# The query rank as the first seven-product unit, with the sums of x partly on GpSimd and two norms moved into later units

## The chip, the cores and the metric

One core of a Trainium2 chip runs the kernel. The metric is the device time of one execution in microseconds (us). Three runs of the kernel before gave 1342.76, 1343.64 and 1344.71; the median is 1343.64. A difference under 0.2% (2.7 us) is about what a measurement of this kernel cannot tell from no change.

## The reference

A hybrid encoder block over 512 tokens of width 2048, float32 throughout. The part that the change touches is the input projection and the two norms that follow it:

```
h = rmsnorm(x, norm_w)
proj = h @ w_in                       # 2048 x 10128
a_q, a_f, a_i, a_g, c_q, c_kv, k_idx_raw, w_idx_raw, b_g, m_a, m_b = split(proj)
# widths: 4 x 1024, c_q 512 (queries' rank), c_kv 256, k_idx_raw 128, 16, 1024, 2 x 2048
cq = rmsnorm(c_q, q_norm_w)           # over 512
k_idx = layernorm(k_idx_raw, kidx_norm_w, kidx_norm_b)    # over 128
...                                   # cq and k_idx are used after all the gates are projected
```

## The kernel before

TensorE multiplies in a pair of fp32r numbers: every operand is split into a high part (ScalarE, a copy to fp32r) and a low part (VectorE, the operand minus its high part), and `mm3` issues three matmuls for each product: high by high, high by low, low by high. `split(hi, lo, src)` writes both parts. x is kept transposed and split in `xh` and `xl`, 16 blocks of 128 rows by 512 tokens.

There are two kinds of projection. `feat_job` is the plain one: it loads a block of weights (`wr`, 512 rows of w_in at a time, two raw buffers), splits it into `wh` and `wl`, and runs `mm3` with 512 tokens as the moving side. `pair_job` is a seven-product scheme (Strassen-Winograd) on 2x2 blocks: 512 features by 512 tokens by 256 rows of x for each block of weights. Of the four quarters of x it needs four sums (`s0` to `s7`, one tile for each pair of 128-row blocks, split in two like all else), of the weights four sums (`pair_sums`, lines 158 to 174: three additions on VectorE into `sv`, then the high parts `bh` and `wh` on ScalarE and the low parts `bl` and `wl` on VectorE). `pair_unit` runs eight blocks of 42 matmuls of 256 columns; its seven results stand in seven PSUM banks, and `pair_evac` puts them together: one ScalarE copy of the first product, then seven VectorE additions. The next unit's first product takes the bank that the ScalarE copy frees, its third to seventh those that the additions free.

There is no scheduler: instructions stand on each engine in the order in which the program is written. `prep(i)` prepares weights up to two blocks ahead of the block that TensorE is about to use. `pump()` is called after each 12 matmuls in a plain job and after each block of a pair unit; it issues the stores that are due and takes one step of every generator in `lanes` ("misc", "norm" and others). `load_ahead` issues the load of a weight block on SyncE's queue as soon as one of the two raw buffers is free by program order.

After `start()` (norm of x, transposes, the values of one head pair) the jobs come in this order: the first half of the queries' rank (`cq_evac(0)`, plain), the raw indexer keys (`kx_evac`), the second half of the rank, the keys' and values' rank (`ckv_evac`), then 13 seven-product units: 11 for the gates and 2 for `qf_d`. Beside the four plain jobs run `pair_gen`, which makes the eight `s` tiles (one pair in three pumps), and on the "norm" lane `q_sums` and `kidx_gen`, the sums of squares by a matmul with ones (`ns`) and the norms' factors (`rstd_row`: Ln and Exp on ScalarE, each behind a table load). `q_rows` scales and splits the rank later, in the third unit. The pools "norms" and "pairs" follow each other in the same memory: `open_pairs` finishes the two lanes and changes the pool when the first pair block is prepared.

Of the kernel before, what the change touches and what calls it, by code (L numbers as in the profile page):

```python
# [63 lines left out]
EVEN = 0  # L64
MO = (0, 128, 384, 768)
# [3 lines left out]
def hybrid_block(ctx, tc, x, norm_w, w_in, lb_table, gnorm_a, q_norm_w, kv_norm_w, w_uq,  # L69
# [51 lines left out]
    cq_d = dram.tile([4, 128, T], F32, name="cq_d")  # L121
    qf_d = dram.tile([2, 4, 128, T], F32, name="qf_d")
# [400 lines left out]
    def cq_evac(j0):  # L523
        def evac(c, ps):
            t = R.cq[:, j0 + c, :]
            A.activation(t, ps, AF.Copy)
            late[1].append(lambda: SP.dma_start(cq_d[j0 + c], t))
        return evac

    def kx_evac(c, ps):  # L530
        A.activation(R.kx[:, 0, :], ps, AF.Copy)

    def ckv_evac(c, ps):
        t = R.g.tile([128, 2, 256], F32, name=f"c{c}").rearrange("p a b -> p (a b)")
        A.activation(t, ps, AF.Copy)
        late[1].append(lambda: SP.dma_start(ckv_d[c], t))
# [7 lines left out]
    def q_sums(j0):  # L544

        for j in (j0, j0 + 1):
            s = R.i.tile([128, T], F32, name="nsq", bufs=2)
            A.activation(s, R.cq[:, j, :], AF.Square)
            if j == 0:
                R.qs = R.i.tile([128, T], F32, name="qs")  # L550
                first = s
            elif j == 1:
                V.tensor_add(R.qs, first, s)
            else:
                V.tensor_add(R.qs, R.qs, s)
        if j0 == 0:
            yield
            return
        sh = R.i.tile([128, T], FR, name="sumh")
        sl = R.i.tile([128, T], FR, name="suml")  # L560
        split(sh, sl, R.qs)
        yield
        yield
# [555 lines left out]
    def open_norms():  # L1119
# [8 lines left out]
        R.cq = R.i.tile([128, 4, T], F32, name="cq")  # L1128
        R.kx = R.i.tile([128, 1, T], F32, name="kx")
# [14 lines left out]
    def pair_gen():  # L1144
        for k in range(8):
            s = slice(2 * (k % 2), 2 * (k % 2) + 2)
            a = R.i.tile([128, 2, T], F32, name="sv", bufs=2)
            V.tensor_tensor(a, xh[k // 2][:, s, :].bitcast(F32), xl[k // 2][:, s, :].bitcast(F32), op=OP.add)
            a11, a21, a12, a22 = (a[:, i, j:j + 256] for i in (0, 1) for j in (0, 256))
            d = R.i.tile([128, 4, 256], F32, name="sv", bufs=2)  # L1150
# [14 lines left out]
            if k == EVEN:  # L1165
                split(hi4, lo4, df[:, 768:])
# [499 lines left out]
```

## Time and profile before

| | |
|---|---|
| median of three runs | 1343.64 us (1342.76 to 1344.71) |
| the profiled execution | 1345.55 us, span of its instructions 1343.8 us |
| TensorE busy | 1331.4 us, 99% of the span |
| VectorE busy | 1088.4 us, 81% |
| ScalarE busy | 691.4 us, 51% |
| GpSimd busy | 51.7 us, 4%; none between 1.6 and 624 us |
| DMA | 150 GB/s, 202.10 MB |
| first plain job starts | 42.43 us |
| first seven-product unit starts | 120.40 us |
| thirteenth ends | 616.12 us |

Times are in us from the first instruction. A busy share is that of instructions in flight; matmuls overlap, so a TensorE at 99% has no wait, but says nothing of the time of one matmul. That is read from the length of a job divided by its matmuls.

### The profile page before, as it was taken

How to read it: one execution, taken by the hardware profiler on the slowest of the kernel's cores; microseconds unless marked ns; L12 is line 12 of the kernel's file. 1: busy time of each engine (PE TensorE's matmuls, PEld its weight loads, DVE VectorE, ACT ScalarE, POOL GpSimd, SP SyncE). 2: the span in 40 equal slices, each digit the busy share in tenths (PEclk: the TensorE clock that was granted, in tenths of full speed). 3: DMA queues.
4: the chain of work that ended last, by engine and by line, in shares of the span. 5: the costliest groups of instructions: out<-in, count | busy, mean ns of one | idle time of the engine just before them, and what ended most of it. 6: DMA issues, size and time to landing. Idle time of an engine off the chain costs nothing.

```text
span 1343.8 us, 27088 instructions
## 1 busy us (share of the span) xinstructions
PE 1331.4 (99%) x11058; PEld 1243.0 (93%) x11058; DVE 1088.4 (81%) x1764; ACT 691.4 (51%) x1115; POOL 51.7 (4%) x63
## 2 busy tenths in 40 slices
PE   8999999999999999999999999999999999999997
PEld 8888999999999999999999898888888888899996
DVE  7978889988898888886778887975656658899997
ACT  7555445545554445445756554655433434354455
POOL 0000000000000000000000000020101100001112
PEclk9999999999999999999999999999999999999999
DMA  7245345544453454446214433445856556654643
GB/s 226 71 118 145 108 142 173 158 141 142 127 154 105 138 154 142 143 143 207 85 51 140 132 106 96 126 136 172 289 167 202 181 187 212 212 174 148 194 145 126
DMA packets 143326, 202.10 MB, mean 150 GB/s; under 512 B 10545, under 2 KB 83810, under 8 KB 143074
## 3 DMA queue, kind: packets, MB, share of 16 engines
q1 hardware_dynamic: 142914, 200.12, 47.5%
q8 instruction: 86, 1.41, 0.4%
q14 instruction: 38, 0.31, 0.1%
q10 hardware_dynamic: 288, 0.26, 0.1%
HBM read 166.25 MB, written 35.66 MB: 150 GB/s over the span
## 4 chain that ended last, share of the span: by engine, by line
PE 97%; DVE 1%; DMA 0%; ACT 0%; issue 0%; SPq 0%; DVEq 0%; ACTq 0%
PE pp L94 16%; PE pp L95 16%; PE pp L96 16%; PE acc L94 14%; PE acc L96 13%; PE acc L95 13%; PE acc L99 2%; PE hl L99 1%; PE ho L99 1%; PE sc L94 1%; PE sc L95 1%; PE sc L96 1%; DMA x<-in_x_dram 0%; PE pt L374 0%; PE hp L99 0%; PE po L96 0%
## 5 line engine op out<-in xcount | busy, mean ns | idle before, releaser
L171 ACT ACTIVATE wh<-sv 128x512 fp32r<-128x512 f32 x264 | 158.6, 625 | 114.4 <-DVE sv L164 85.4
L169 ACT ACTIVATE bh<-wr 128x768 fp32r<-128x768 f32 x132 | 111.5, 845 | 197.6 <-issue 91.8
L95 PE MATMUL pp<-s,wh 128*128 128x256 f32 x624 | 172.6, 277 | 0.0
L94 PE MATMUL pp<-s,wh 128*128 128x256 f32 x624 | 172.6, 277 | 0.0
L96 PE MATMUL pp<-s,wl 128*128 128x256 f32 x624 | 172.6, 277 | 0.0
L173 DVE TENSOR_TENSOR wl<-sv,wh 128x1024 fp32r<-128x1024 f32 x132 | 161.2, 1221 | 5.4
L172 DVE TENSOR_TENSOR bl<-wr,bh 128x768 fp32r<-128x768 f32 x132 | 126.0, 954 | 37.7 <-ACT bh L169 37.3
L94 PE MATMUL acc<-xh,wh 128*128 128x512 f32 x304 | 121.0, 398 | 0.0
L96 PE MATMUL acc<-xh,wl 128*128 128x512 f32 x304 | 118.8, 391 | 0.0
L95 PE MATMUL acc<-xl,wh 128*128 128x512 f32 x304 | 118.6, 390 | 0.0
L95 PEld LDWEIGHTS pp<-s,wh 128*128 128x128 f32 x624 | 117.2, 188 | 0.0
L96 PEld LDWEIGHTS pp<-s,wl 128*128 128x128 f32 x624 | 117.2, 188 | 0.0
L94 PEld LDWEIGHTS pp<-s,wh 128*128 128x128 f32 x624 | 117.2, 188 | 0.0
L95 PE MATMUL pp<-xl,bh 128*128 128x256 f32 x416 | 115.1, 277 | 0.0
L96 PE MATMUL pp<-xh,bl 128*128 128x256 f32 x416 | 115.0, 277 | 0.0
L94 PE MATMUL pp<-xh,bh 128*128 128x256 f32 x416 | 115.0, 277 | 0.0
L91 DVE TENSOR_TENSOR wl<-wr,wh 128x1024 fp32r<-128x1024 f32 (+1 forms) x70 | 84.0, 1201 | 28.8 <-ACT wh L90 28.7
L90 ACT ACTIVATE wh<-wr 128x1024 fp32r<-128x1024 f32 (+1 forms) x70 | 72.3, 1033 | 61.6 <-PE acc L95 38.1
L164 DVE TENSOR_TENSOR sv<-wr 128x512 f32<-128x512 f32 x132 | 92.7, 702 | 10.3 <-DMA wr<-in_w_in_dram 6.9
L94 PE MATMUL acc<-yh,wh 128*128 128x512 f32 x256 | 100.3, 392 | 0.0
L96 PE MATMUL acc<-yh,wl 128*128 128x512 f32 x256 | 99.9, 390 | 0.0
L95 PE MATMUL acc<-yl,wh 128*128 128x512 f32 x256 | 99.9, 390 | 0.0
(391 smaller groups left out, 3769.9 us busy)
## 6 DMA issues: line engine op xcount, KB each, us to landing
wr<-in_w_in_dram SPq DMA_DIRECT2D x136, 512.0 KB, 3.7
wr<-in_w_out_dram SPq DMA_DIRECT2D x28, 512.0 KB, 3.9
mg<-gate_d SPq DMA_DIRECT2D x48, 256.0 KB, 5.3
gate_d<-c SPq DMA_DIRECT2D x44, 256.0 KB, 5.2
wr<-in_w_in_dram SPq DMA_DIRECT2D x36, 256.0 KB, 3.1
wr<-in_w_pa_dram SPq DMA_DIRECT2D x16, 512.0 KB, 5.4
wr<-in_w_pb_dram SPq DMA_DIRECT2D x16, 512.0 KB, 4.0
wr<-in_w_qidx_dram SPq DMA_DIRECT2D x8, 512.0 KB, 4.5
```

The costliest lines, as they stand in the source:

```text
L90: A.activation(hi, src, AF.Copy)
L91: V.tensor_tensor(lo, src, hi.bitcast(F32), op=OP.subtract)
L94: PE.matmul(ps, lh, rh, start=first, stop=False, skip_group_check=True)
L95: PE.matmul(ps, lh, rl, start=False, stop=False, skip_group_check=True)
L96: PE.matmul(ps, ll, rh, start=False, stop=last, skip_group_check=True)
L99: PE.matmul(ps, l, r, start=first, stop=last, skip_group_check=True)
L164: V.tensor_tensor(sv[:, 0:2, :], b[:, 1:3, :], b[:, 0:1, :].to_broadcast([128, 2, 256]), op=OP.add)
L169: A.activation(bh, b[:, 1:4, :], AF.Copy)
L171: A.activation(vh[:, i:i + 2, :], sv[:, i:i + 2, :], AF.Copy)
L172: V.tensor_tensor(bl, b[:, 1:4, :], bh.bitcast(F32), op=OP.subtract)
L173: V.tensor_tensor(vl, sv, vh.bitcast(F32), op=OP.subtract)
```

## The change

The four plain jobs of 256, 128, 256 and 256 features become two, the keys' and values' rank and the indexer keys; the queries' rank (512 features) becomes the first seven-product unit, ahead of the thirteen. `pair_gen` becomes two generators. `pair_early` makes six of the eight `s` tiles beside the two plain jobs, one pair in each pump: VectorE adds the two parts of x (`xa`) and makes the first sum, GpSimd makes the other three (`G.tensor_tensor`, 256 columns), and the split follows two steps later. `pair_late` makes the last two beside the first two blocks of the rank's unit, with two of four sums on GpSimd. The raw indexer keys go through memory (`kx_d`). `kidx_gen` and a new `q_squares` (which reads the rank back from `cq_d` to square and add it) run in the units after, followed by `q_rows`.

```diff
+EARLY = 6
...
     def kx_evac(c, ps):
-        A.activation(R.kx[:, 0, :], ps, AF.Copy)
+        t = R.g.tile([128, 2, 256], F32, name="c0").rearrange("p a b -> p (a b)")
+        A.activation(t, ps, AF.Copy)
+        SP.dma_start(kx_d, t)
...
+    def q_squares():
+        for j0 in (0, 2):
+            for _ in range(3):
+                yield
+            ts = [R.g.tile([128, 2, 256], F32, name=f"c{i}").rearrange("p a b -> p (a b)") for i in range(2)]
+            for i, t in enumerate(ts):
+                SP.dma_start(t, cq_d[j0 + i])
+            yield
+            yield
+            for t in ts:
+                A.activation(t, t, AF.Square)
...
+        sh, sl = R.cqh[:, 3, :], R.cql[:, 3, :]
+        split(sh, sl, R.rq)
+        yield
+        ps = row_sums(sh, sl)
+        rstd_row(ps, 512, R.rq)
+        for _ in range(7):
+            yield
...
     def kidx_gen():
+        t, parts = R.rq, (R.cqh[:, 2, :], R.cql[:, 2, :])
+        SP.dma_start(t, kx_d)
+        yield
+        yield
+        split(*parts, t)
+        yield
+        ps = row_sums(*parts)
+        V.scalar_tensor_tensor(t, ps, -1.0 / 128, t, op0=OP.mult, op1=OP.add)
+        yield
+        s = R.g.tile([128, 2, 256], F32, name="c3").rearrange("p a b -> p (a b)")
         A.activation(s, t, AF.Square)
+        split(*parts, s)
+        yield
+        rstd_row(row_sums(*parts), 128, s)
+        yield
+        V.scalar_tensor_tensor(t, t, c_iw, s, op0=OP.mult, op1=OP.mult)
         V.tensor_scalar(t, t, c_ib, None, op0=OP.add)
         split(R.kih, R.kil, t)
...
+    def pair_early():
+        made = []
+        for k in range(EARLY + 2):
+            if k > 1:
+                hi, hi4, lo, lo4 = sums_place(k - 2)
+                df = made.pop(0).rearrange("p q n -> p (q n)")
+                split(hi, lo, df[:, 0:768] if hi4 is not None else df)
...
+            if k < EARLY:
+                a = R.i.tile([128, 2, T], F32, name="xa", bufs=3)
+                V.tensor_tensor(a, *pair_rows(k), op=OP.add)
+                a11, a21, a12, a22 = (a[:, i, j:j + 256] for i in (0, 1) for j in (0, 256))
+                d = R.i.tile([128, 4, 256], F32, name="sv", bufs=3)
+                V.tensor_tensor(d[:, 0, :], a21, a22, op=OP.subtract)
+                G.tensor_tensor(d[:, 1, :], d[:, 0, :], a11, op=OP.subtract)
+                G.tensor_tensor(d[:, 2, :], a11, a21, op=OP.subtract)
+                G.tensor_tensor(d[:, 3, :], d[:, 1, :], a12, op=OP.add)
+                made.append(d)
+            yield
+
+    def pair_late():
+        for k in range(EARLY, 8):
+            ae, ao, da, db = (R.g.tile([128, 2, 256], F32, name=f"c{i}") for i in range(4))
+            for i, a in enumerate((ae, ao)):
+                V.tensor_tensor(a.rearrange("p a b -> p (a b)"), *(x[:, i, :] for x in pair_rows(k)), op=OP.add)
+            a11, a21, a12, a22 = (a[:, j, :] for a in (ae, ao) for j in (0, 1))
+            V.tensor_tensor(da[:, 0, :], a21, a22, op=OP.subtract)
+            V.tensor_tensor(da[:, 1, :], da[:, 0, :], a11, op=OP.subtract)
+            G.tensor_tensor(db[:, 0, :], a11, a21, op=OP.subtract)
+            G.tensor_tensor(db[:, 1, :], da[:, 1, :], a12, op=OP.add)
+            yield
+            hi, _, lo, _ = sums_place(k)
...
-    lane("misc", pair_gen)
-    feat_job(w_in, 4096, 2, NK, 4, x_rhs, cq_evac(0))
-    lane("norm", lambda: q_sums(0))
+    lane("misc", pair_early)
+    feat_job(w_in, 4608, 2, NK, 4, x_rhs, ckv_evac)
     feat_job(w_in, 4864, 1, NK, 4, x_rhs, kx_evac)
-    lane("norm", kidx_gen)
-    feat_job(w_in, 4352, 2, NK, 4, x_rhs, cq_evac(2))
-    lane("norm", lambda: q_sums(2))
-    feat_job(w_in, 4608, 2, NK, 4, x_rhs, ckv_evac)
+    lane("misc", pair_late)
+    pair_job(w_in, [4096, 4352], NK // 2, x_pair, pair_evac([cq_d[0:2], cq_d[2:4]], [None, None]))
+    for gen in (kidx_gen, q_squares, q_rows):
+        lane("norm", gen)
```

Line numbers move by two in the helpers: the split's low part is line 91 before and 92 after, the three matmuls 94 to 96 and 95 to 97. In the rows that follow, `wl<-wr,wh` is the low part of a weight block, `s<-sv,s` that of a sum of x, and `sv<-xh,xl` or `xa<-xh,xl` the two parts of x added.

The first place is VectorE from the first sum of x on, beside the first plain job. Before:

```order
L1148 TENSOR_TENSOR sv<-xh_92,xl_95 128x1024
L1151 TENSOR_TENSOR sv<-sv 128x256
L91 TENSOR_TENSOR wl<-wr,wh 128x1024
L1153 TENSOR_TENSOR sv<-sv 128x256
L1154 TENSOR_TENSOR sv<-sv 128x256
L1155 TENSOR_TENSOR sv<-sv 128x256
L91 TENSOR_TENSOR s_713<-sv,s_713 128x768
L91 TENSOR_TENSOR s_713<-sv,s_713 128x256
L91 TENSOR_TENSOR wl<-wr,wh 128x512
```

After, from the fourth pair's `xa` to the low part of the last block of the indexer keys:

```order
L1167 TENSOR_TENSOR xa<-xh_94,xl_97 128x1024
L1170 TENSOR_TENSOR sv<-xa 128x256
L92 TENSOR_TENSOR s_771<-sv,s_771 128x1024
L1167 TENSOR_TENSOR xa<-xh_92,xl_95 128x1024
L1170 TENSOR_TENSOR sv<-xa 128x256
L92 TENSOR_TENSOR wl<-wr,wh 128x512
L92 TENSOR_TENSOR s_801<-sv,s_801 128x1024
L1167 TENSOR_TENSOR xa<-xh_92,xl_95 128x1024
L1170 TENSOR_TENSOR sv<-xa 128x256
L92 TENSOR_TENSOR s_826<-sv,s_826 128x1024
L92 TENSOR_TENSOR wl<-wr,wh 128x512
L92 TENSOR_TENSOR s_849<-sv,s_849 128x1024
```

Three of four 256-column sums of a pair have left VectorE, and the weights' low parts of the indexer keys (128x512) now stand behind the sums of five and six pairs, where one or two stood ahead of them. The row behind the last is again `wl<-wr,wh 128x512`.

On GpSimd, whose queue held nothing between the start and the cast for the branches, stand the sums of the first pair, and the same three rows for each of the next five:

```order
L336 MEMSET rows 128x128
L1171 ISA
L1171 TENSOR_TENSOR sv<-sv,xa 128x256
L1172 TENSOR_TENSOR sv<-xa 128x256
L1173 TENSOR_TENSOR sv<-sv,xa 128x256
```

They came from VectorE's lines 1153 to 1155.

The second place is VectorE in the rank's unit, behind the weights of its third block (`sv<-wr` to `wl<-sv,wh` are one block's weights; `c` tiles hold the two halves of x and their sums, `s_1063` is the seventh pair's place):

```order
L1181 TENSOR_TENSOR c_996<-xh_92,xl_95 128x512
L1181 TENSOR_TENSOR c_997<-xh_92,xl_95 128x512
L1183 TENSOR_TENSOR c_998<-c_996,c_997 128x256
L1184 TENSOR_TENSOR c_998<-c_998,c_996 128x256
L166 TENSOR_TENSOR sv<-wr 128x512
L167 TENSOR_TENSOR sv<-sv,wr 128x256
L168 TENSOR_TENSOR sv<-sv,wr 128x256
L174 TENSOR_TENSOR bl<-wr,bh 128x768
L175 TENSOR_TENSOR wl<-sv,wh 128x1024
L92 TENSOR_TENSOR s_1063<-c_998,s_1063 128x512
L92 TENSOR_TENSOR s_1063<-c_999,s_1063 128x512
```

In units before only the five rows from `sv<-wr` on stood there; the four above and the two below are new, once for each of the two late pairs.

The third place is ScalarE in the first gate unit, from the sixth block on. Before, two blocks' weights (`bh`, `wh`) and the evacuation's copy (`c<-pp`):

```order
L169 ACTIVATE bh<-wr 128x768
L171 ACTIVATE wh<-sv 128x512 x2
L169 ACTIVATE bh<-wr 128x768
L171 ACTIVATE wh<-sv 128x512 x2
L1222 ACTIVATE c_1710<-pp 128x512
```

After:

```order
L537 ACT_TABLE_LOAD
L537 ACTIVATE c_1740<-ns,cols 128x512
L538 ACT_TABLE_LOAD
L538 ACTIVATE c_1740<-c_1740 128x512
L171 ACTIVATE bh<-wr 128x768
L173 ACTIVATE wh<-sv 128x512 x2
L91 ACTIVATE kih<-rq 128x512
L171 ACTIVATE bh<-wr 128x768
L173 ACTIVATE wh<-sv 128x512 x2
L1243 ACTIVATE c_1922<-pp 128x512
```

The factor of the indexer keys' norm, which stood beside the plain jobs, now stands ahead of the high parts of the next two weight blocks. It waits for the `ns` matmuls behind the unit's sixth block. Behind those weights on VectorE stand the norm's last three operations (lines 631, 632 and the low part `kil`), ahead of the unit's evacuation.

More of the change, by code (lines that the diff above doesn't have):

```diff
@@ L542, in rstd_row, with row_sums @@
         return r
[L544 to L553, printed above, removed]
-            else:
-                V.tensor_add(R.qs, R.qs, s)
-        if j0 == 0:
-            yield
[L558 to L563, printed above, removed]
+    def q_squares():
[9 more added lines that the diff above has]
+                A.activation(t, t, AF.Square)
+            if j0 == 0:
+                V.tensor_add(R.rq, *ts)
+            else:
+                V.tensor_add(ts[0], *ts)
+                V.tensor_add(R.rq, R.rq, ts[0])
+            for _ in range(3):
+                yield
[5 more added lines that the diff above has]
+        for _ in range(7):
+            yield
+    def row_sums(sh, sl):
         ps = bank("ns")
@@ new lines, in sums_place @@
+    def sums_place(k):
+        t = R.x.tile([128, 2048 + 64 * (k == EVEN)], FR, name=f"s{k}")
+        if k == EVEN:
+            parts = [t[:, 0:768], t[:, 784:1040], t[:, 1344:2112], t[:, 1040:1296]]
+        else:
+            parts = [t[:, 0:1024], None, t[:, 1024:2048], None]
+        for xs, a, b in ((xs_h, *parts[0:2]), (xs_l, *parts[2:4])):
+            cut = [a[:, i:i + 256] for i in range(0, 768, 256)]
+            xs.append(cut + [a[:, 768:1024] if b is None else b])
+        return parts
@@ new lines, in pair_rows @@
+    def pair_rows(k):
+        return (x[k // 2][:, 2 * (k % 2):2 * (k % 2) + 2, :].bitcast(F32) for x in (xh, xl))
+    def pair_early():
[5 more added lines that the diff above has]
+                split(hi, lo, df[:, 0:768] if hi4 is not None else df)
+                if hi4 is not None:
+                    split(hi4, lo4, df[:, 768:])
+            if k < EARLY:
[8 more added lines that the diff above has]
+                made.append(d)
+            yield
@@ new lines, in pair_late @@
+    def pair_late():
[8 more added lines that the diff above has]
+            G.tensor_tensor(db[:, 1, :], da[:, 1, :], a12, op=OP.add)
+            yield
+            hi, _, lo, _ = sums_place(k)
+            for i, d in enumerate((da, db)):
+                n = slice(i * 512, i * 512 + 512)
+                split(hi[:, n], lo[:, n], d.rearrange("p a b -> p (a b)"))
@@ L1231, in store @@
                 def store(c=c, f=f, t=t):
-                    A.activation(c, c, fn[f])
+                    if fn[f] is not None:
+                        A.activation(c, c, fn[f])
                     late[1].append(lambda: SP.dma_start(dst[f][:, :, t:t + 256].rearrange("f p t -> p f t"), c))
```

57 lines of the change are left out of this document (3 added, 54 removed).

## The prediction

> **What bounds the kernel now.** I read the page first, for the share of each engine and the chain that ended last:
>
> ```profile
> PE 1331.4 (99%) x11058; PEld 1243.0 (93%) x11058; DVE 1088.4 (81%) x1764; ACT 691.4 (51%) x1115; POOL 51.7 (4%) x63
> PE 97%; DVE 1%; DMA 0%; ACT 0%; issue 0%; SPq 0%; DVEq 0%; ACTq 0%
> ```
>
> TensorE never waits for long, so a matmul less is time less as long as the others keep up. Then the windows by stage: the first rank half, the indexer keys, the second half, the first unit and the third (the one with `q_rows`):
>
> ```profile
> core 0: us, PE busy (x) PEld busy (x) DVE busy (x) ACT busy (x) POOL busy (x), PEclk, DMA share, GB/s
> 42.43:64.21 21.78, 21.78 (x99) 18.04 (x97) 18.96 (x38) 10.43 (x18) 0.00 (x0) 1.00 0.25 64
> 64.21:75.10 10.89, 10.89 (x50) 9.03 (x49) 8.94 (x14) 5.98 (x8) 0.00 (x0) 1.00 0.58 171
> 75.10:97.90 22.80, 22.80 (x102) 18.84 (x101) 16.65 (x24) 13.09 (x16) 0.00 (x0) 1.00 0.39 112
> 120.40:158.53 38.13, 38.13 (x336) 38.12 (x335) 33.13 (x47) 18.69 (x30) 0.00 (x0) 1.00 0.51 149
> 196.66:234.80 38.14, 38.14 (x338) 38.14 (x337) 35.59 (x52) 19.11 (x32) 0.00 (x0) 1.00 0.50 153
> ```
>
> A plain job of 256 features takes 21.78 us for 96 matmuls (0.227 each), a unit 38.13 for 336 (0.1135 each, 4.77 a block). VectorE is busy for 33.13 of a unit's 38.13: it follows closely, and its queue, not its share, must be read next. The timeline of VectorE where the sums of x begin:
>
> ```profile
> 52.81 1.22 DVE L1148 TENSOR_TENSOR sv<-xh,xl 128x1024 f32<-128x1024 f32 x1
> 54.06 0.42 DVE L1151 TENSOR_TENSOR sv<-sv 128x256 f32<-128x256 f32 x1
> 54.41 1.22 DVE L91 TENSOR_TENSOR wl<-wr,wh 128x1024 fp32r<-128x1024 f32 x1
> 55.54 0.42 DVE L1153 TENSOR_TENSOR sv<-sv 128x256 f32<-128x256 f32 x1
> 57.20 1.29 DVE L91 TENSOR_TENSOR s<-sv,s 128x768 fp32r<-128x768 f32 x2 [0.45 <-ACT s L90]
> 58.42 0.68 DVE L91 TENSOR_TENSOR wl<-wr,wh 128x512 fp32r<-128x512 f32 x1
> 59.02 1.22 DVE L1148 TENSOR_TENSOR sv<-xh,xl 128x1024 f32<-128x1024 f32 x1
> ```
>
> Steps from start to start: 1.13 us for 1024 columns, 0.60 for 512, 0.35 for 256, 1.22 for 768 with 256, and 1.60 for `xa` with the sum that reads it. And VectorE at the end of the first unit (which ends at 158.53):
>
> ```profile
> 156.44 0.69 DVE L1223 TENSOR_TENSOR c<-pp,c 128x512 f32<-128x512 f32 x1
> 159.16 0.68 DVE L1227 TENSOR_TENSOR c<-pp,c 128x512 f32<-128x512 f32 x1
> 160.96 0.68 DVE L164 TENSOR_TENSOR sv<-wr 128x512 f32<-128x512 f32 x1
> 162.48 0.95 DVE L172 TENSOR_TENSOR bl<-wr,bh 128x768 fp32r<-128x768 f32 x1
> 163.35 1.22 DVE L173 TENSOR_TENSOR wl<-sv,wh 128x1024 fp32r<-128x1024 f32 x1
> 164.48 0.68 DVE L164 TENSOR_TENSOR sv<-wr 128x512 f32<-128x512 f32 x1
> ```
>
> One pair block of weights takes 3.52 (160.96 to 164.48), 2.39 of it to the end of `bl`; the evacuation takes 4.52 and begins 2.1 before the unit's end. The next unit's fifth product takes the bank that the fifth addition (L1227) frees. It is due 24 matmuls into the unit, at 158.53 + 2.72 = 161.25, and the addition ends at 159.84: 1.4 us of slack.
>
> **Matmuls.** Removed: two plain jobs, 2 x 21.78 = 43.56 (the 1.0 more of the second window are four `ns` matmuls, which only move). Added: one unit, 38.13. That is -5.43 us, all of it on the path, if TensorE isn't kept waiting. The rank's stores stay four; its evacuation and the two table loads of each norm stay in number.
>
> **VectorE up to the rank's unit.** Number the weight blocks 0 to 3 (keys' and values' rank), 4 to 7 (indexer keys), 8 to 15 (rank's unit), 16 on (gates). Up to 52.81 nothing changes. TensorE needs a low part at a block's third matmul: block 5 at 64.21 + 2.72 + 0.45 = 67.4, block 6 at 70.1, block 7 at 72.8; the `bl` of pair block 12 at 75.1 + 4 x 4.77 + 0.23 = 94.4. Ahead of block 7's low part VectorE now has six `xa` with their sum (6 x 1.60), the low parts of six sums (1.22 + 5 x 1.13) and five blocks (1.13 + 4 x 0.60): 20.0, so 72.8. Just in time, if GpSimd's 18 sums cost VectorE nothing.
>
> They don't come free. Where GpSimd's adds met VectorE late in this trace:
>
> ```profile
> 878.82 1.89 POOL L1012 TENSOR_TENSOR MB<-M,bh 128x256 f32<-128x256 f32 x2 [49.64 <-DMA bh<-bh_d]
> 878.86 1.25 DVE L816 TENSOR_TENSOR hq<-hq,tot 128x512 f32<-128x512 f32 x1
> 880.04 1.22 DVE L818 TENSOR_TENSOR hk<-hk,tot 128x512 f32<-128x512 f32 x1
> 880.68 0.90 POOL L1014 TENSOR_TENSOR MB<-M,bh 128x128 f32<-128x128 f32 x1
> 881.18 1.47 DVE L91 TENSOR_TENSOR wl<-wr,wh 128x1024 fp32r<-128x1024 f32 x1
> 881.54 1.72 POOL L1012 TENSOR_TENSOR MB<-M,bh 128x256 f32<-128x256 f32 x1
> 882.58 1.29 DVE L828 TENSOR_TENSOR tot<-tot 128x256 f32<-128x256 f32 x2
> 883.78 0.69 DVE L816 TENSOR_TENSOR hq<-hq,tot 128x512 f32<-128x512 f32 x1
> ```
> ```profile
> L1012 POOL TENSOR_TENSOR MB<-M,bh x24: 727/738/1721, 878.8 to 1060.3; 128x256 f32<-128x256 f32 x24
> ```
>
> The two take turns: L816 takes 1.25 beside a 256-column add, 0.69 without; L818, of the same shape, 1.22. Each such add stops VectorE for 0.53 to 0.56 us, more than the 0.35 that VectorE would need for the sum itself, and is stopped in turn (738 ns alone, up to 1721). I take 0.53, the lower, since some adds will fall into VectorE's own waits; the ends are 0, and 0.74 (the whole add).
>
> The Trainium skill's page "SBUF — State Buffer", section "Who interferes with whom", says that a VectorE instruction with two SBUF inputs and a GpSimd instruction that reads SBUF exclude each other, and that the loser blocks for the whole instruction. By that the cost would be 0.74 an add; the rows above show less, 0.53 to 0.56, and I go by them.
>
> So 18 x 0.53 = 9.5 on top. Walked down the queue, with one GpSimd add between every two VectorE operations: block 5's low part at 73.6 (6.2 us late), block 6's at 80.25 (3.9 more), then VectorE waits 1.1 for ScalarE's high part of the sixth sum, and block 7's is done at 83.7. The load of block 8 waits for block 6's low part (the raw buffer):
>
> ```profile
> wr<-in_w_in_dram SPq DMA_DIRECT2D x136, 512.0 KB, 3.7
> ```
>
> With 0.4 to issue it lands at 84.3. From there four blocks (14.1), the VectorE part of the two late pairs (2 x 2.0), the low parts of the seventh (1.2), block 12 to its `bl` (2.4) and four more adds (2.0): 108.0, against 94.4. TensorE is 13.6 us late. Without the stops the same walk gives block 6 at 70.95 (0.85 late), block 7 at 74.2, block 8's load at 75.0, and 96.7 for block 12: 2.3 us.
>
> **Unit boundaries.** From block 12 on VectorE has 1.1 + 1.2 (eighth pair) + 5 x 3.52 = 19.9 before the evacuation, TensorE 18.8 to the unit's end: the evacuation begins 1.1 after the end instead of 2.1 before it. Less the slack of 1.4 this holds the next unit for 1.8 us.
>
> In the first gate unit (blocks 16 to 23) the keys' norm meets the same edge. Its factor waits for `ns` matmuls behind block 21; the chain on ScalarE is that of the rank's norm before:
>
> ```profile
> 109.57 1.28 ACT L540 ACT_TABLE_LOAD   x1
> 110.86 0.69 ACT L540 ACTIVATE rq<-ns,cols 128x512 f32<-128x512 f32 x1
> 111.57 1.28 ACT L541 ACT_TABLE_LOAD   x1
> 112.86 0.63 ACT L541 ACTIVATE rq<-rq 128x512 f32<-128x512 f32 x1
> ```
>
> Behind it stand the high parts of block 24, which otherwise start when block 21 is done:
>
> ```profile
> L169 ACT ACTIVATE bh<-wr 128x768 fp32r<-128x768 f32 x132 | 111.5, 845 | 197.6 <-issue 91.8
> ```
>
> Counted from the end of block 21: the factor at 3.95, `bh` of block 24 at 4.8, its two low parts on VectorE (0.9 and, behind the last `wh`, 1.1) at 7.2, the norm's last three operations at 0.6 each with ScalarE's 0.6 between them 9.6, block 25 13.1. Then the evacuation, and the unit ended at 9.5. That is 3.6 late, and 3.6 + 2.1 - 1.4 = 4.3 us of waiting. Bounds: 0, if the operations slip into gaps, and 6.5 (all that stands on ScalarE and VectorE for it). I take 4.3. `q_squares` has its factor early in the third gate unit, where 1.25 us a block are left over to make it good, and its three additions and split fit beside 33.13; hidden, at most 1 us if the cover goes. Six more loads and stores on SyncE: at a DMA share of 0.5 hidden; the stores of raw keys stand behind one ScalarE copy, with block 11's load behind them, which has 3 us to spare.
>
> **The sum.** -5.43 + 13.6 + 1.8 + 4.3 = +14.3. The profiled execution took 1345.55 (span 1343.8, 1.75 around it), 1.9 above the median; it would take 1359.8, and the median of 1343.64 becomes 1357.9 us.
>
> **Rivals.** (1) GpSimd is free. It runs only in VectorE's waits: 2.3 + 1.8 + 4.3 - 5.43 = +3.0, 1346.6. The rows above speak against it: VectorE has hardly a wait here. (2) Faster: GpSimd is free and the evacuations aren't late, because VectorE fits the norm's operations ahead: -5.43 + 2.3 = -3.1, 1340.5. It decides at 0.14 us an add, (5.43 - 2.3) / 22; below that the change wins. (3) The stops as forecast but no wait at the gates' edge: 1351.8. (4) More: 22 adds at 0.74 give +4.6, 1362.5. Or the clock falls in the long waits. At the kernel's end, after the last matmul at 1336.2, it does:
>
> ```profile
> 1336.00:1338.00 2.00, 0.19 (x2) 0.00 (x0) 0.89 (x3) 0.81 (x3) 0.00 (x0) 1.00 0.86 320
> 1338.00:1340.00 2.00, 0.00 (x0) 0.00 (x0) 1.14 (x3) 1.12 (x2) 0.00 (x0) 0.55 0.21 78
> ```
>
> About 2 us of idleness halve it, and the waits of 6.2 and 3.9 are longer. Blocks 6 and 7 at half speed are 24 x 0.227 = 5.4 more; VectorE, late itself, hides 2.2 of it (block 8's `bl` is done at 84.3 + 2.4 = 86.7 against 75.3, so TensorE is 11.4 late there, and 13.6 at block 12): +3.2, 1361.1. The Trainium skill's "TensorE: Matmul & The Clock Gate", section "What's actually happening", puts the drop after an idle window of about 3.4 us; by that the 6.2 would halve the clock and the 3.9 perhaps not, and the sum would stay at the forecast.
>
> **How the numbers follow.** The forecast 0.55, its own range 1352 to 1361; (3) 0.08; (1) 0.12, which lies on the edge of 0.2% (2.7 us, about what a measurement tells from no change), so I halve it; (2) 0.13; (4) 0.12. Slower: 0.55 + 0.08 + 0.12 + 0.06 = 0.81; same 0.06; faster 0.13. The range reaches from 1343 (leaving out the faster case) to 1363 (past both of (4)).
>
> **What would show it.** VectorE operations on `xa` and `s` at 1.6 to 1.8 us instead of 1.22, GpSimd adds over 1 us; TensorE waiting for `wl` in the indexer keys, some 10 us between 67 and 84; then for `bl` in the rank's unit, and at the starts of the first and second gate unit for the evacuation. The rank's unit should end near 127 (75.1 + 38.1 + 13.6). I am wrong if the adds run at 0.74 and VectorE at 1.22, or if GpSimd finishes within VectorE's waits.

## The result: 15 us slower, and the profile after

The changed kernel takes 1359.53 us (median of four runs, 1358.20 to 1360.15), the kernel before on the same chip 1344.18 (1342.76 to 1344.88): a ratio of 1.0114, 95% interval 1.0097 to 1.0132. The profiled execution took 1358.2 us, its span is 1356.4. Three single runs, one of experiment 1 (1473.53 us) and two of the kernel before (2233.47 and 4754.76), fell in a slow state of the chip and count in no median or ratio below.

From the page of the changed kernel, the shares of the engines and the chain that ended last:

```profile
PE 1333.1 (98%) x11202; PEld 1249.7 (92%) x11202; DVE 1110.2 (82%) x1785; ACT 701.3 (52%) x1131; POOL 78.8 (6%) x85
PE 92%; DVE 4%; ACT 1%; POOL 1%; issue 0%; DMA 0%; SPq 0%; DVEq 0%; ACTq 0%; POOLq 0%
```

Before, TensorE was 97% of that chain; now VectorE holds 4% of it and GpSimd 1%. Where TensorE waited between 42 and 260 us, for what, and in how many pieces (us in total, times, longest; `acc` is a plain job's accumulator, `pp` a product of a seven-product unit):

```profile
PE acc L97 <- DVE wl L92: 4.8, 2, 3.1
PE acc L95 <- ACT wh L91: 3.8, 2, 2.3
PE pp L95 <- ACT c L1243: 3.1, 1, 3.1
PE pp L95 <- DVE c L1248: 0.8, 1, 0.8
PE pp L97 <- DVE bl L174: 0.6, 1, 0.6
```

The first two rows (8.6 us) lie in the indexer keys' blocks 5 and 6. The third is the edge between the first two gate units (L1243 is the evacuation's ScalarE copy), the fourth the edge between the rank's unit and the first gate unit (L1248 is the fifth addition), the fifth is block 12. The windows of TensorE by stage: the keys' and values' rank, the indexer keys, the rank's unit, the first three gate units, and two short stretches behind the two long waits:

```profile
core 0: us, PE busy (x) PEld busy (x) DVE busy (x) ACT busy (x) POOL busy (x), PEclk, DMA share, GB/s
41.31:64.10 22.79, 22.79 (x103) 18.86 (x101) 20.82 (x33) 9.42 (x16) 8.94 (x8) 1.00 0.17 47
64.10:88.08 23.98, 15.33 (x45) 10.86 (x44) 19.78 (x20) 9.62 (x13) 13.19 (x11) 0.72 0.30 87
88.08:127.97 39.89, 39.30 (x338) 39.09 (x337) 39.12 (x58) 21.35 (x34) 4.38 (x4) 1.00 0.43 126
127.97:171.50 43.53, 39.61 (x343) 39.07 (x341) 35.50 (x54) 22.42 (x34) 0.00 (x0) 1.00 0.43 128
171.50:211.25 39.75, 39.75 (x337) 39.75 (x338) 35.90 (x53) 21.58 (x33) 0.00 (x0) 0.96 0.52 159
211.25:249.37 38.12, 38.12 (x339) 38.12 (x338) 34.25 (x50) 19.04 (x32) 0.00 (x0) 1.00 0.51 153
72.43:76.00 3.57, 3.57 (x9) 2.84 (x10) 3.54 (x3) 0.00 (x0) 3.57 (x3) 0.55 0.49 147
80.42:84.00 3.58, 3.58 (x9) 2.81 (x10) 1.83 (x2) 1.01 (x2) 0.00 (x0) 0.50 0.67 171
```

The two plain jobs take 46.77 us where 144 matmuls at 0.2269 need 32.67: 14.1 lost. The rank's unit loses 1.8 against the 38.12 of an undisturbed unit, the first gate unit 4.5 (its 0.92 of `ns` matmuls taken off), the second 1.6. That is 22.0, less 5.43 for the matmuls and 0.34 for the `ns` work (1.40 us instead of 1.74): 16.2 us. Counted directly, from the first plain job to the end of the last unit, it is 16.0. The two profiled executions differ by less, 12.65 us, since that of before was 1.4 above its median of 1344.18 and that of after 1.3 below; in the trace, after starts the jobs 1.1 us earlier and is 2.3 us shorter behind the seven-product units. By the medians it is 15.35.

VectorE's groups between 50 and 84 us (shape, count, busy us, mean ns, idle time before them), and GpSimd's in the same stretch:

```profile
L1167 DVE TENSOR_TENSOR xa<-xh,xl 128x1024 f32<-128x1024 f32 x6 | 10.0, 1662 | 0.0
L92 DVE TENSOR_TENSOR s<-sv,s 128x1024 fp32r<-128x1024 f32 x5 | 8.3, 1667 | 2.3 <-ACT s L91 2.3
L1170 DVE TENSOR_TENSOR sv<-xa 128x256 f32<-128x256 f32 x6 | 3.8, 633 | 0.2
L1173 POOL TENSOR_TENSOR sv<-sv,xa 128x256 f32<-128x256 f32 x6 | 8.7, 1447 | 0.0
L1171 POOL TENSOR_TENSOR sv<-sv,xa 128x256 f32<-128x256 f32 x6 | 5.9, 986 | 56.1 <-DVE sv L1170 54.4 <-ACT ck L532 1.7
```

The 1024-column additions, 1.22 us before, take 1.66 in the mean: 1.74 to 1.76 where a GpSimd add met them, which is five of the six. GpSimd's adds take up to 1.73 us in their turn. VectorE also waits for the sums' high parts, which ScalarE makes from what GpSimd delivers (us in total, times, longest):

```profile
DVE s L92 <- ACT s L91: 2.9, 4, 0.8
```

### The profile page after: what moved, and what is told of

The parts are those of the page before. It is cut to its first block, busy times and chain, and to the rows that moved or that the text cites. A ratio compares the mean times of both kernels' runs of the same rounds, so it can differ in the third digit from the quotient of the medians.

```text
span 1356.4 us, 27477 instructions
## 1 busy us (share of the span) xinstructions
PE 1333.1 (98%) x11202; PEld 1249.7 (92%) x11202; DVE 1110.2 (82%) x1785; ACT 701.3 (52%) x1131; POOL 78.8 (6%) x85
## 4 chain that ended last, share of the span: by engine, by line
PE 92%; DVE 4%; ACT 1%; POOL 1%; issue 0%; DMA 0%; SPq 0%; DVEq 0%; ACTq 0%; POOLq 0%
PE pp L95 16%; PE pp L96 16%; PE pp L97 16%; PE acc L95 12%; PE acc L97 12%; PE acc L96 12%; PE hl L100 1%; PE ho L100 1%; PE acc L100 1%; DVE xl L389 1%; PE sc L95 1%; PE sc L96 1%; PE sc L97 1%; DMA x<-in_x_dram 0%; DVE s L92 0%
## 5 line engine op out<-in xcount | busy, mean ns | idle before, releaser
L173 ACT ACTIVATE wh<-sv 128x512 fp32r<-128x512 f32 x280 | 170.0, 626 | 146.1 <-DVE sv L166 113.5
L95 PE MATMUL pp<-s,wh 128*128 128x256 f32 x672 | 185.9, 277 | 0.8 <-DVE c L1248 0.8
L96 PE MATMUL pp<-s,wh 128*128 128x256 f32 x672 | 185.7, 276 | 0.0
L97 PE MATMUL pp<-s,wl 128*128 128x256 f32 x672 | 185.7, 276 | 0.0
L175 DVE TENSOR_TENSOR wl<-sv,wh 128x1024 fp32r<-128x1024 f32 x140 | 171.0, 1221 | 4.4
L95 PE MATMUL pp<-xh,bh 128*128 128x256 f32 x448 | 124.5, 278 | 3.1 <-ACT c L1243 3.1
L95 PEld LDWEIGHTS pp<-s,wh 128*128 128x128 f32 x672 | 126.3, 188 | 1.0 <-issue 1.0
L96 PEld LDWEIGHTS pp<-s,wh 128*128 128x128 f32 x672 | 126.4, 188 | 0.0
L97 PE MATMUL pp<-xh,bl 128*128 128x256 f32 x448 | 124.4, 278 | 0.6 <-DVE bl L174 0.6
L95 PE MATMUL acc<-xh,wh 128*128 128x512 f32 x240 | 97.6, 407 | 3.8 <-ACT wh L91 3.8
L97 PE MATMUL acc<-xh,wl 128*128 128x512 f32 x240 | 95.8, 399 | 4.8 <-DVE wl L92 4.8
L96 PE MATMUL acc<-xl,wh 128*128 128x512 f32 x240 | 95.2, 396 | 0.0
```

The source lines that it names most:

```text
L95: PE.matmul(ps, lh, rh, start=first, stop=False, skip_group_check=True)
L96: PE.matmul(ps, lh, rl, start=False, stop=False, skip_group_check=True)
L97: PE.matmul(ps, ll, rh, start=False, stop=last, skip_group_check=True)
L173: A.activation(vh[:, i:i + 2, :], sv[:, i:i + 2, :], AF.Copy)
L175: V.tensor_tensor(vl, sv, vh.bitcast(F32), op=OP.subtract)
```

## The experiments

Each was timed against the kernel before on its own chip (medians of 1342.8 to 1343.4 us in those runs), so ratios to before are compared. "Late" is meant of TensorE.

**1. All sums on VectorE.** Five lines of `pair_early` and `pair_late`:

```diff
-                G.tensor_tensor(d[:, 1, :], d[:, 0, :], a11, op=OP.subtract)
+                V.tensor_tensor(d[:, 1, :], d[:, 0, :], a11, op=OP.subtract)
... (so in all five)
```

> The changed kernel with all of its GpSimd adds (18 in the three early sums of six pairs, 4 in the two late pairs) issued on VectorE, nothing else changed. Theory A (each add on GpSimd stops VectorE for 0.53 us, more than the 0.35 it needs to do the sum itself): 22 x 0.18 = 4.0 us come back, about 1355.5 us (1352 to 1357.5), VectorE's operations on xa and s back at 1.22, TensorE's waits for wl of the indexer keys' blocks shorter by about 3 us. Rival B (GpSimd's adds are free and VectorE is late by its own work alone): VectorE gets 22 x 0.35 = 7.7 us more, and the time rises to about 1367.

Measured: 1355.17 us, ratio 1.0091 (1.0077 to 1.0105). By the number it is theory A: VectorE does 22 additions more and the kernel gets 3.1 (by the ratios to before) to 4.4 us faster (by the medians). The intervals of the two ratios overlap a little; the single runs do not (1354.72 to 1355.47 against 1358.20 to 1360.15). The same VectorE groups in this run:

```profile
L1167 DVE TENSOR_TENSOR xa<-xh,xl 128x1024 f32<-128x1024 f32 x6 | 7.3, 1217 | 0.0
L1171 DVE TENSOR_TENSOR sv<-sv,xa 128x256 f32<-128x256 f32 x6 | 2.6, 426 | 0.2
```

By the mechanism it is theory A only in part. In the changed kernel GpSimd's adds stretch VectorE's operations beside the plain jobs by 7.75 us (added up below, in the part on the prediction); here VectorE does these 18 additions itself, and by its timeline a pair's three take 1.13 us, all of them 6.8. That is 1.0 us less, not 18 x 0.18 = 3.2. The larger part are the 2.9 us in which VectorE waited for the high parts of the sums; this run has no such wait. Together they fit the 3.7 us by which TensorE passes block 12 earlier, counted from the first plain job. In the changed kernel GpSimd's three adds, one behind the other, stand on the chain that ended last, between VectorE's first sum and the low part (start, us, what):

```profile
62.27 1.12 POOL sv L1171
63.40 1.68 POOL sv L1172
65.08 1.67 POOL sv L1173
66.77 1.07 ACT s L91
67.86 1.79 DVE s L92
```

TensorE's waits for `wl` are not 3 us shorter, though, but 0.9 longer, 5.7 in all; what went are the 3.8 for `wh`:

```profile
PE acc L97 <- DVE wl L92: 5.7, 2, 4.7
```

**2. GpSimd writes, but doesn't read.** The sums that GpSimd made are left out.

```diff
-                G.tensor_tensor(d[:, 1, :], d[:, 0, :], a11, op=OP.subtract)
+                G.memset(d[:, 1, :], 0.0)
... (so in all five)
```

> The changed kernel with each GpSimd add replaced by a memset of the same tile on GpSimd: it writes and reads nothing. Three of the four sums of x of six pairs, and two of the two late pairs, are thereby left out, so the output is not the reference's; VectorE's and TensorE's instructions are the same in number and shape. Theory A (GpSimd's reads stop VectorE, 0.53 us each): VectorE's 1024-column operations come back from 1.75 to 1.22 us, TensorE is late by about 2 to 3 us at block 12 instead of 13.6, about 1348 us (1345 to 1351). Rival B (VectorE is late by its own added work): 1357 to 1360. Rival C (GpSimd's writes stop VectorE too): VectorE's operations stay above 1.5 us and the time stays above 1354.

Measured: 1346.57 us, ratio 1.0026 (1.0015 to 1.0037). Theory A. VectorE's additions run at their undisturbed time, and the kernel is 12 to 13 us faster than the changed one. In these groups, from 50 to 84 us:

```profile
L1167 DVE TENSOR_TENSOR xa<-xh,xl 128x1024 f32<-128x1024 f32 x6 | 7.3, 1219 | 0.0
L1171 POOL MEMSET sv<- 128x256 f32 x3 | 0.9, 315 | 19.0 <-DVE s L92 19.0
```

Nine of the 18 early memsets run between 57.4 and 64.4 us, beside three of the six additions, and each of the three takes 1.22 us. The other nine had to wait for nothing that VectorE makes and ran at 40 to 43 us, ahead of the sums. VectorE does not wait for a high part in this run either, so it takes away the stops and the lateness of GpSimd's chain together and does not weigh one against the other; the trace of the changed kernel does that (7.75 and 2.9 us).

The Trainium skill's "SBUF — State Buffer", section "Who interferes with whom", says that a VectorE instruction with two SBUF inputs contends with a GpSimd instruction that reads SBUF, and not with one that only writes. By these two runs the trace agrees on that. The section also calls it an exclusive lock; the size here is less than the whole instruction: an add that takes 0.72 us alone stops VectorE for 0.53.

**3. The keys' norm six blocks later.**

```diff
     def kidx_gen():
+        for _ in range(6):
+            yield
...
         split(R.kih, R.kil, t)
-        yield
-        yield
+        for _ in range(4):
+            yield
```

> The changed kernel with the indexer keys' norm started six blocks later (and two idle steps more at its end, so that the queries' norm keeps its place in a unit, one unit later): its factor, with the two table loads, falls behind the fourth block of the second gate unit instead of two blocks ahead of the edge between the first two. Theory A (the factor stands ahead of the next high parts on ScalarE and makes the evacuation late): the last block of the first gate unit goes from 8.0 to about 4.8 us, and the half clock in the block after it (1.6 us) goes too: -4.9, about 1354.6 us (1353 to 1357). Rival B (the norm's work holds the units wherever it stands): 1358.5 to 1360.5, the wait only moves one unit on.

Measured: 1360.85 us, ratio 1.0137 (1.0122 to 1.0151). Theory A fell. The first edge is clean (blocks of 4.76 and 4.80 in place of 8.01 and 6.43), but the second gate unit pays it back: its fourth block takes 6.52, its last 6.83, and the block after the next edge 6.44. The move made a new wait. The norm's square goes to the tile `c3`, which the evacuation had just used, and ScalarE stands until its store has landed. ScalarE's rows on that and the VectorE row behind it:

```profile
186.73 0.63 ACT L628 ACTIVATE c<-rq 128x512 f32<-128x512 f32 x1 [3.31 <-DMA gate_d<-c]
188.06 0.69 DVE L92 TENSOR_TENSOR cql<-c,cqh 128x512 fp32r<-128x512 f32 x1 [3.30 <-ACT cqh L91]
```

So this run does not decide the question; run 5 does.

**4. TensorE's clock kept up in the two long waits.**

```diff
+                if ntile == 1 and i in (1, 2):
+                    wm = bank("wm")
+                    for _ in range((0, 20, 11)[i]):
+                        PE.matmul(wm[:, 0:128], ones, ones, start=True, stop=True)
```

> The changed kernel with extra 128 x 128 matmuls on spare data into a spare bank, 20 ahead of block 5 and 11 ahead of block 6 of the indexer keys, so that TensorE does not idle in its two long waits there. Theory A (VectorE is late by the same amount whatever TensorE does, since its low part of block 8 is done at 87 and that of block 12 near 108): the plain blocks run at full clock, but the gain is given back in waits in the rank's unit: 1358.5 to 1360. Rival B (the half clock behind the waits costs what it lasts): 5.4 us of slow matmuls in the plain blocks and 1.6 in the rank's unit come back, about 1353 to 1356.

Measured: 1359.11 us, ratio 1.0122 (1.0106 to 1.0138). Theory A. The clock is up, in the indexer keys' blocks and after (64 to 88 us), and the rank's unit starts 2.6 us earlier:

```profile
64.00:74.00 10.00, 8.47 (x58) 7.44 (x57) 9.09 (x9) 3.60 (x5) 7.89 (x7) 1.00 0.13 30
74.00:88.00 14.00, 10.67 (x61) 8.69 (x60) 10.70 (x12) 6.00 (x8) 5.36 (x5) 1.00 0.43 129
```

but then TensorE waits 2.9 us for `bl` at blocks 8 and 12, in place of 0.6, and goes on from block 12 at 108.29 us, where the changed kernel went on at 108.31:

```profile
PE pp L97 <- DVE bl L174: 2.9, 2, 1.7
```

The half clock cost nothing here: it filled time that TensorE would have spent waiting for VectorE. By the trace of the changed kernel the same holds at the start of the second gate unit, where the first block takes 1.6 us more than usual at a granted clock of 0.56. The fifth addition and the first matmul of the fifth product, which needs its bank:

```profile
174.93 0.68 DVE L1248 TENSOR_TENSOR c<-pp,c 128x512 f32<-128x512 f32 x1
175.78 0.34 PE L95 MATMUL pp<-s,wh 128*128 128x256 f32 x1
```

The addition ends at 175.61 and the product starts at 175.78. At full clock it would have been due 24 matmuls (2.7 us) after the unit's start at 171.50, at 174.2, and would have waited. In run 3 the block after the later edge ran at full clock and took 6.44 us as well, 1.1 of them in a wait for this addition. So the 1.6 us are the late evacuation's and not the clock's, to which the expectations of runs 3 and 4 put them down.

**5. The keys' norm four blocks later, without `c3`.**

```diff
     def kidx_gen():
+        for _ in range(4):
+            yield
...
-        s = R.g.tile([128, 2, 256], F32, name="c3").rearrange("p a b -> p (a b)")
+        s = bank("ns")
         A.activation(s, t, AF.Square)
...
-        rstd_row(row_sums(*parts), 128, s)
+        s = row_sums(*parts)
+        rstd_row(s, 128, s)
... (and four idle steps more at its end)
```

> The changed kernel with the keys' norm four blocks later and without the evacuation's tile c3: its square and its factor are kept in the spare PSUM bank, so that nothing waits for a store (in the run with the six-block shift ScalarE waited 3.3 us for the store of c3 and the factor came four blocks ahead of a unit's end). The factor now comes behind the second block of the second gate unit, six blocks ahead of the edge. Theory A (a factor's 5 us without high parts are made good at 1.25 us a block, so the place decides and the two-block distance was the fault): 1354 to 1356 us, the last block of the first gate unit and the first of the second at 4.8 each, no wait elsewhere. Rival B (VectorE has no room for the norm in any unit): the wait moves to the next edge again, 1358.5 to 1361.

Measured: 1357.1 us, ratio 1.0102 (1.0089 to 1.0116), between the two theories: 1.6 to 2.4 us gained instead of 4.9, so little that the intervals of the two ratios overlap. The edge and the block behind it are clean (5.22, of which 0.46 is `ns`, and 4.82), so the place of the factor was the fault at that edge. But the second gate unit takes 40.33 and not 38.12. Its second block takes 5.83: 0.46 of `ns`, a short wait ahead of it, since the square stands behind four Silu stores on ScalarE, and the restart. And its other six blocks take 4.95 each instead of 4.76, with matmuls at 0.118 us for 0.1134, no wait and a granted clock of 1.00. What slows those stays open; the changed kernel has three such blocks at the end of the rank's unit.

**6. Both mends** (runs 1 and 5 together).

> Both mends at once: all sums of x on VectorE, and the keys' norm four blocks later with square and factor in PSUM. Theory A (two separate terms, which add): 1355.4 less 4.9, about 1350.5 us (1349 to 1352.5), still slower than before since VectorE is late by its own work ahead of the rank's unit. Rival B (the terms share one lateness): above 1353.

Measured: 1353.39 us, ratio 1.0074 (1.0062 to 1.0087). The number is rival B's (above 1353), but not for B's reason: theory A's 1350.5 counted on a gain of 4.9 in run 5, which gave less. By the ratios 3.1 of run 1 and 1.6 of run 5 make 4.7, and 5.4 were measured, so the two terms add as far as these runs can tell. The six slow blocks of run 5 take 4.76 us each here.

**7. Sums from the unsplit x.** On top of run 6, `start()`'s tiles `y` stay in a pool of their own until the seven-product units' pool is opened (the pools of the rank and the keys move behind it, which makes the room).

```diff
-                a = R.i.tile([128, 2, T], F32, name="xa", bufs=3)
-                V.tensor_tensor(a, *pair_rows(k), op=OP.add)
+                a = R.ys[k // 2][:, 2 * (k % 2):2 * (k % 2) + 2, :]
... (the pools; the second and third sum change places)
```

> Both mends, and the six early sums of x made from the unsplit x of the start stage, kept in a pool of its own, instead of from high part plus low part: six additions of 1024 columns (1.13 us each) fall away, and the second and third sum are issued in the other order (0.1 us each). Theory A (what TensorE waits for up to block 12 is VectorE's queue, one for one): 7.4 us less than with both mends, about 1343 us (1340 to 1345), so no worse than the kernel before. Rival B (block 8's load or ScalarE's high parts are late next): 1346 to 1350.

Measured: 1346.4 us, ratio 1.002 (1.0011 to 1.0029): 7.0 less than run 6 for 7.4 us of VectorE's work. Up to the rank's unit TensorE now waits 0.15 us, one for one as theory A has it, yet the time is at the lower end of rival B's range. What is late next is block 8's load: VectorE finishes its sums and stands. The last low part of the plain blocks, and the first operation of block 8:

```profile
70.70 0.68 DVE L92 TENSOR_TENSOR wl<-wr,wh 128x512 fp32r<-128x512 f32 x1
73.83 0.69 DVE L166 TENSOR_TENSOR sv<-wr 128x512 f32<-128x512 f32 x1 [2.45 <-DMA wr<-in_w_in_dram]
```

**8. GpSimd's adds in the kernel before.** Three of four sums of `pair_gen` moved to GpSimd, 24 adds:

```diff
-            V.tensor_tensor(d[:, 2, :], a11, a21, op=OP.subtract)
+            G.tensor_tensor(d[:, 2, :], a11, a21, op=OP.subtract)
... (so the next two)
```

> The kernel before with the last three sums of each of its eight pairs on GpSimd (24 adds) instead of VectorE. Theory A (each add stops VectorE for 0.53 us in place of 0.35 us of work, but VectorE has 1 us a plain block to spare there): VectorE's operations beside them stretch to about 1.75 us, and TensorE waits little or not: 1343 to 1346 us. Rival B (GpSimd's adds cost the time of the kernel wherever they stand): 24 x 0.18 = 4.3 us, 1347 to 1348. Rival C (GpSimd frees VectorE): 1342 to 1343.

Measured: 1349.26 us, ratio 1.0048 (1.0035 to 1.006), above all three ranges and nearest to B, though not by B's even cost per add. I had counted TensorE's waits for low parts alone. What is late here is the norm's chain, which stands in the same two queues, and the clock is down behind that wait (0.50 from 110.5 to 114.0 us):

```profile
PE ns L99 <- ACT sumh L90: 2.8, 1, 2.8
PE ns L99 <- DVE suml L91: 0.8, 1, 0.8
```

So GpSimd's adds cost the kernel before 5.9 us with nothing else changed.

**9 and 10. One plain job of 384 features**, on top of run 7: eight blocks of 768 columns, in place of two jobs, with one step of the sums behind each block; seven pairs early (9) or all eight (10).

```diff
-    feat_job(w_in, 4608, 2, NK, 4, x_rhs, ckv_evac)
-    feat_job(w_in, 4864, 1, NK, 4, x_rhs, kx_evac)
+    feat_job(w_in, 4608, 3, NK, 2, x_rhs, keys_evac)
... (one evacuation for the three parts; EARLY = 7 or 8)
```

> The kernel with both mends and sums from the unsplit x, and further: the keys' and values' rank and the indexer keys as one plain job of 384 features in eight blocks of 256 rows (768 columns each) with one step of the sums behind each block, in place of four blocks of 1024 columns and four of 512; the seventh pair's sums are early too, so one pair is left for the rank's unit. Theory A (what is left over the ideal is VectorE's order: block 8's load is issued late because block 6's low part stands behind the sums in VectorE's queue, and 1.6, 1.7 and 1.7 us follow at blocks 8 and 12 and at the unit's end): VectorE no longer idles 2.4 us for block 8's load, block 8's low part is at most 1.5 us late and block 12's on time, about 1341.5 us (1340 to 1344), below the kernel before. Rival B (the waits at the gates' edges set it whatever is ahead): 1345 to 1347, the rank's unit shorter and the second gate unit's end later.

> The kernel with one plain job, with all eight pairs' sums early. VectorE has 2.5 us more ahead of block 8 and 3.7 less in the rank's unit. Theory A (VectorE's queue, one for one): block 8's low part about 3.5 to 4 us late, nothing later: 1343 to 1345 us, some 2 us above the one with seven early. Rival B (the waits at the gates' edges set it): 1345 to 1347, as with seven early.

Measured: 1351.46 us, ratio 1.0063 (1.005 to 1.0077), and 1355.44 us, ratio 1.0084 (1.0068 to 1.0099); the single runs spread over 4.5 and 5.3 us. Both theories missed in both runs. The waits of run 9:

```profile
PE acc L95 <- DVE widx L412: 3.1, 1, 3.1
PE pp L95 <- ACT c L528: 2.4, 1, 2.4
PE pp L97 <- DVE bl L174: 1.9, 1, 1.9
```

I had counted VectorE's time and not the PSUM banks. Three accumulators at once need a bank that the start stage still holds (its last reader is the copy to `widx`), and the rank's unit needs, right at its start, the banks that three ScalarE copies have to free. And with one step of the sums a block, VectorE stood for 3.4 us at one low part, whose high part had to wait for TensorE to give its place free, with the sums queued behind it. The rank's unit itself, with one late pair or none, ran without a wait behind its first block: that part I kept.

**11 and 12. Seven pairs early, then the norm in two parts.** Run 7 (its two plain jobs as in the change), and

```diff
-EARLY = 6
+EARLY = 7
...
-        for k in range(EARLY + 2):
-            if k > 1:
-                hi, hi4, lo, lo4 = sums_place(k - 2)
+        for k in range(EARLY + 3):
+            if k > 2:
+                hi, hi4, lo, lo4 = sums_place(k - 3)
```

and in run 12 also

```diff
         V.scalar_tensor_tensor(t, t, c_iw, s, op0=OP.mult, op1=OP.mult)
+        for _ in range(8):
+            yield
```

> The kernel with both mends and sums from the unsplit x (two plain jobs as in the changed kernel), with the seventh pair early too and the low parts of the sums one step later (three steps behind their sums in place of two), so that block 6's low part, which frees block 8's raw buffer, stands behind four low parts of sums and not five. Theory A (VectorE's order and its idle 2.4 us ahead of block 8): block 8's low part stays about 1.5 us late, the 1.7 at block 12 and the 1.7 at the rank's unit's end go, since 3.7 us less stands in that unit: 3 us less than the run with six early, about 1343 us (1341.5 to 1344.5). Rival B (block 8's load gets later, or another edge takes the wait): 1346 to 1349.

> As the run with seven early, and the last two steps of the keys' norm (bias, high and low part) eight blocks later than its product, in the third gate unit. Theory A (the norm's work on VectorE behind the factor is what is not made good by the end of the second gate unit): the evacuation there is on time, 1.4 to 1.7 us less than the run with seven early, about 1341.5 us (1340 to 1343.5), under the kernel before. Rival B (the factor's own 4 us on ScalarE is what holds that unit's end): as the run with seven early, within 0.5 us.

Measured: 1342.56 us, ratio 0.9994 (0.9985 to 1.0003), and 1339.4 us, ratio 0.9973 (0.9962 to 0.9983). Theory A in both. Run 12 came out 0.6 below its range: besides the edge behind the second gate unit (6.22 to 4.80 in the block after it) two later units, 38.35 and 39.19 us in run 11, take 38.12, since the queries' norm, too, moved on by a unit. Why it meets those two edges in run 11 and none in run 12 stays open. Run 12 is 3.6 to 3.9 us faster than the kernel before, and 19 to 20 faster than the change as it was made. TensorE's share and its waits there, and the stages (plain jobs, rank's unit, three gate units):

```profile
PE 1324.6 (99%) x11202; PEld 1243.7 (93%) x11202; DVE 1099.1 (82%) x1798; ACT 701.4 (52%) x1130; POOL 52.5 (4%) x63
PE pp L97 <- DVE bl L174: 1.0, 1, 1.0
PE acc L97 <- DVE wl L92: 0.5, 1, 0.5
PE ns L100 <- DVE cql L92: 0.3, 1, 0.3
74.34:113.72 39.38, 38.41 (x338) 38.21 (x337) 38.65 (x58) 22.14 (x34) 0.00 (x0) 1.00 0.48 138
113.72:152.30 38.58, 38.58 (x341) 38.50 (x339) 34.62 (x51) 17.16 (x27) 0.00 (x0) 1.00 0.49 151
152.30:191.52 39.22, 38.88 (x340) 38.59 (x339) 33.43 (x50) 24.82 (x36) 0.00 (x0) 1.00 0.46 133
191.52:229.63 38.11, 38.11 (x338) 38.11 (x337) 33.88 (x51) 20.50 (x32) 0.00 (x0) 1.00 0.47 140
```

Of the 22 us that the change lost to waits and slow stretches in these stages, under 3 are left: 0.7 in the plain jobs, 1.3 in the rank's unit, 0.6 in the second gate unit beside its `ns` matmuls. So the -5.43 of the matmuls was there all the time; it was covered.

## Why the prediction was right, point by point

- **Matmuls, -5.43.** Held: an undisturbed unit takes 38.12, and with the waits out (run 12) most of it shows.
- **GpSimd's adds stop VectorE, 0.53 each.** Held, and with the lateness of GpSimd's own chain the step that decided: run 2, without both, is 12 to 13 us faster. Where an add meets a 1024-column addition this takes 1.75 in place of 1.22. Not every add meets one: VectorE's operations beside the plain jobs are stretched by 7.75 us for 18 adds, 0.43 in the mean, where I counted 9.5 (2.7 in the six `xa`, 3.3 in the low parts of the sums, 1.25 in the first sums, 0.5 in the low parts of the weights). VectorE's waits for ScalarE's high parts of the sums, which come late because GpSimd's adds take so long, are 2.9 where I counted 1.1. That the two errors cancel, 10.65 against 10.6, is luck.
- **VectorE's walk.** With the jobs starting 1.1 us earlier than in the profile that I walked in, it gave 72.5 for block 5's low part, 79.1 for block 6's, 82.6 for block 7's, 83.2 for block 8's load and 106.9 for block 12. They came at 72.4, 80.4, 82.8, 84.5 and 108.3. The term of 13.6 is mis-sized by 1.4: TensorE is 15.0 late at block 12. It is lost between blocks 5 and 6, in VectorE's waits for the high parts, and the load behind block 6 carries it on.
- **The edges.** 1.8 was forecast for the first; its block takes 1.2 more than the usual 4.80, and the three slow blocks ahead of it 0.6, which is time that it would have waited: in runs 2, 3 and 4, which lack them, this edge costs 2.0. For the second 4.3 was forecast; it costs 3.25 in the last block and 1.6 in the next, 4.9. Of that 3.1 are a wait that the prediction did not work out, for ScalarE's copy (L1243), which stands behind the same late high parts; but the fifth addition, from which the 4.3 was worked out, still ends last. The chain behind it is the one forecast: the factor's two table loads on ScalarE from 159.23 us, behind them block 24's high part, behind that VectorE, which had stood for 5.15 us:

```profile
159.23 1.28 ACT L537 ACT_TABLE_LOAD   x1 [3.32 <-PE ns L100]
163.06 0.83 ACT L171 ACTIVATE bh<-wr 128x768 fp32r<-128x768 f32 x1
163.93 0.96 DVE L174 TENSOR_TENSOR bl<-wr,bh 128x768 fp32r<-128x768 f32 x1 [5.15 <-ACT bh L171]
```

- **The sum.** +14.3 forecast; +16.0 in the stages by the trace, +15.35 by the medians. The walk gives 1.4 of the difference to the trace and the second edge 0.6; the `ns` work takes 0.34 off. Two readings of rows were slightly off and move no term by more than 0.15: the first unit of the kernel before ends at 158.68, not 158.53, and `bl` ends 2.47 us into its block, not 2.39.
- **`q_squares` hidden.** Held: its factor falls in the fourth gate unit (I had it in the third), which takes 38.60, 0.48 over the others, and that is its `ns` matmuls.
- **Rival 1, GpSimd free, 1346.6.** Run 2 made it true and gave 1346.57. Its terms are near the rival's and not equal to them: 3.0 at block 12, 2.0 and 4.9 at the two edges, where the rival had 2.3, 1.8 and 4.3; a hit to 0.03 us is luck. **Rival 2** needed on-time edges besides, which run 2 did not have: it still waits 3.1 and 1.1 us there.
- **The clock in rival 4.** It did fall, three times, but its price was wrong. The number alone could not tell: 1359.53 lies 1.6 us from the forecast and 1.6 from this rival's 1361.1. Run 4 decides it. The rival let VectorE hide only 2.2 of 5.4 us; run 4 shows that it hid all. Even by the prediction's own numbers 2.2 was too little: TensorE's two waits make it 6.2 + 3.9 = 10.1 late, with 5.4 of half clock 15.5, against the 13.6 that VectorE sets at block 12, so 1.9 would have shown and not 3.2. The rival had added the 5.4 to the 11.4 of block 8, which already holds 1.3 us of waiting there. In the run the two waits are 8.6, the slow matmuls 5.5, together 14.1, and VectorE sets 15.0 at block 12.

## What to carry to other kernels

Before work is moved to GpSimd, look at what VectorE does in that stretch: if both read two operands from SBUF, a 256-column add on GpSimd cost VectorE 0.53 us where the two met (0.43 in the mean), where doing it itself cost 0.35, and the sums came later, which here cost VectorE another 2.9 us of waiting. A saving on the bound engine counts only as far as the second engine keeps up, so count the second engine's work before and after in the same stretch: here VectorE's work for the sums of x had been spread over four plain jobs, and two of them went. When a wait is taken out, ask what stands next in the same queue, and count the banks and tiles that the moved step needs and not its time alone; runs 3, 7 and 9 missed on that (a tile's store, a raw buffer, a bank of the start stage).

## What the hardware showed unasked

- TensorE's granted clock was 0.56 to 0.58 for 3.5 us behind single waits of 2.8 (run 1) and 3.1 us (the changed kernel), and 1.00 behind one of 1.9 (run 3). Where between 1.9 and 2.8 it turns stays open. The windows behind the waits in run 1 and in run 3:

```profile
168.05:171.60 3.55, 3.55 (x19) 3.55 (x20) 3.41 (x6) 0.68 (x1) 0.00 (x0) 0.58 0.50 148
```
```profile
210.27:214.00 3.73, 3.14 (x24) 2.94 (x24) 3.59 (x6) 0.73 (x1) 0.00 (x0) 1.00 0.48 141
```

- At the half clock the 512-column matmul steps at 0.427 us instead of 0.227. The Trainium skill's "TensorE: Matmul & The Clock Gate", section "What's actually happening", gives an idle window of about 3.4 us for the drop; in run 1 a wait of 2.8 was enough.
- A half clock behind a wait cost nothing where VectorE set the next wait (run 4, and the block after the second edge).
- A VectorE addition of 256 columns that reads the result of the one just before it starts 0.46 us after it, one that doesn't 0.34.
- Beside VectorE a GpSimd add of 256 columns took up to 1.73 us, alone 0.72; a memset of the same tile took 0.315, and the VectorE additions beside it kept their 1.22.
